# A list schedule in place of the framework's scheduler, for a two-layer hybrid backbone on one core

## The chip, the cores and the metric

The kernel runs on one core of one Trainium2 chip. The metric is the device time of one execution in microseconds (us); three runs of the kernel before gave 1246.17, 1247.41 and 1250.1 us, median 1247.41. The engines are TensorE (PE, with its weight loads as PEld), VectorE (DVE), ScalarE (ACT), GpSimd (POOL) and SyncE (SP, whose queue issues every DMA). Each engine executes its own list of instructions in order; semaphores hold an instruction until what it needs is there.

## The reference

Two layers, 640 tokens (512 of a latent grid, 128 of a prompt), width 1024. In each layer:

```python
def layer(x, cvec, lp, lam_init, cache):
    mod = jax.nn.silu(cvec) @ lp['w_mod'] + lp['b_mod']
    shift, scale, gate = jnp.split(mod[:, None, :], 3, -1)
    h = rms_norm(x, lp['g_pre']) * (1.0 + scale) + shift
    y, new_cache = mixer(h, lp, lam_init, cache)
    return x + gate * rms_norm(y, lp['g_post']), new_cache

def mixer(h, lp, lam_init, cache):   # cut
    (ar, ak, av, awd, aad, ag, bq, bk, bv, bg, cx, cg, dq, dk, dv, dg) = split_cols(h @ lp['w_in'])
    ya = rwkv_branch(...)    # RWKV-7, two directions, state per head
    yb = window_latent(...)  # windowed attention with a sink
    yc = rglru_branch(...)   # convolution, gates, linear recurrence, two directions
    yd = diff_attend(...)    # softmax(q1 k1) - lam * softmax(q2 k2)
    return concat(ya * silu(ag), yb * silu(bg), yc * silu(cg), yd * silu(dg)) @ lp['w_out']
```

## The kernel before

Every projection is a sum of three products of float32r matmuls: activations are held as a high and a low part (`HA`, `HB`), weights too (`WP`, `WQ`, `ZA`, `K`); ACT writes the high part (L515), DVE the difference (L518). All matmuls but the transposes are issued by the helper `mm` (L345).

In a layer the program is written in this order. `fm1`: projections that give the RG-LRU input (tiles 4, 5) and the RWKV inputs (8 to 12). `lru` (L997): convolution, gate products, scans, both directions. `rwkv_norm`, then for direction 0 the stages `pre`, `bonus`, `mats`, `ends`, `inv`, `keys`; five `tm_chunk`s (queries, keys and values of the attentions, with the pieces of the modulation between them); `solve` for direction 0; all stages again for direction 1; the windowed attention with four gate tiles (`fm2`, `E_TILES`, L1656 to L1660); `rwkv_chain` (seven dependent steps on the state) and `rwkv_read`; then the differential attention (`diff`), with four more gate tiles (`F_TILES`), the end of RWKV (`rwkv_out`) and the output weights between its steps; at last `out`. `inv` inverts triangular 32x32 blocks by 31 dependent steps shared by POOL and DVE (L1273, L1275), with a way through DRAM before and after. `diff` works on 4 heads of 5 query tiles: packing (L839, L843, L845), scores, a minimum on DVE (L873), exponentials on ACT (L876), a combination on DVE (L881), transposes (L887) and the product with the values.

Tiles stand in hand-placed slots (`SLOTS`, the `M_...` places): a later tile in the same place waits for the last user of the earlier one. Weights come through two buffers (`raw`, `N_RAW = 2`).

The order on each engine is not the written one. The tile framework's scheduler sets it, from its own estimate of times and from priorities: blocks under `first()` (L1703) are moved ahead by 1000 places, the steps of `window` and `diff` by `WP1` and `DP1` (L1693). So the RG-LRU and the RWKV stages stand beside the first projections.

Of the kernel before, what the change touches and what calls it, by code (L numbers as in the profile page):

```python
# [10 lines left out]
F32 = mybir.dt.float32  # L11
F32R = mybir.dt.float32r
# [9 lines left out]
NT = 5  # L22
# [236 lines left out]
class Net:  # L259
    def __init__(self, tc, es, I, O, dbg=None):  # L260
        self.tc, self.nc, self.I, self.O = tc, tc.nc, I, O
        self.dbg = dbg or {}
        nc = tc.nc
        self.V, self.A, self.G, self.P = nc.vector, nc.scalar, nc.gpsimd, nc.tensor
        self.pool = es.enter_context(tc.tile_pool(name="sb", bufs=1))
        self.ps = es.enter_context(tc.tile_pool(name="ps", bufs=1, space=PSUM))
        self.dram = es.enter_context(tc.tile_pool(name="dr", bufs=1, space=bass.MemoryType.DRAM))
        self.slots = {}
        self.banks = self.ps.tile([128, 8, 512], F32, name="banks")
        self.n = 0  # L270
        self.rot = {}
        self.sm_tag = "sm"
# [5 lines left out]
    def sb(self, shape, tag, bufs=1, dt=F32):  # L278

        self.n += 1  # L280
        return self.pool.tile(list(shape), dt, tag=tag, bufs=bufs, name=f"{tag}_{self.n}")

    def new(self, *slots, dt=F32):

        for k in slots:
            self.n += 1
            self.slots[k] = dt, self.pool.tile([128, round(SLOTS[k] * U)], dt, tag=k, bufs=1, name=f"{k}_{self.n}")

    def at(self, place, shape, dt=F32):

# [228 lines left out]


    def raw(self):
        self.n += 1
        return self.pool.tile([128, RAW], F32, tag="raw", bufs=N_RAW, name=f"raw_{self.n}")

    def weight(self, pieces, hi, lo):

# [1209 lines left out]
```

## Time and profile before

| | |
|---|---|
| median of three runs | 1247.41 us (1246.17 to 1250.1) |
| profiled execution | 1240.3 us, its span 1238.4 us |
| PE busy | 1078.4 us (87%) |
| DVE, ACT, POOL busy | 727.2, 518.0, 385.5 us |
| mean granted TensorE clock | 0.902 of full speed |

The span runs from the first to the last instruction. Busy is the time in which an engine executes something; matmuls are pipelined, so the duration of one matmul in a row is longer than the distance to the next one. PEclk is the granted clock, 1.00 at 2.4 GHz and 0.50 at 1.2 GHz, averaged over a stretch. The views used are: the page's shares, the chain of waits (work followed back from the last instruction), windows (busy time in chosen stretches), and the timeline (instructions in order of time, equal neighbours merged, with the idle time before a row and its releaser in brackets).

### The profile page before, as it was taken

The page shows a single profiled execution, that of the slowest core. Times are in us where ns is not written, and L with a number is a line of the kernel's source. Part 1 is how long each engine was busy: PE and PEld are TensorE (multiplying, and loading weights), DVE is VectorE, ACT ScalarE, POOL GpSimd, SP SyncE. Part 2 cuts the span into 40 slices and gives each one's busy share as a digit, 9 for nine tenths or more (in the row PEclk, how much of TensorE's full clock was granted, in tenths as well). Part 3 has the DMA queues.
Part 4 walks back from the last instruction along what each step waited for, and adds up shares of the span by engine and source line. Part 5 has one row for each costly group of instructions (what it writes and reads, how often), then busy time and mean ns, then how long its engine had stood idle before and what let it go on. Part 6 is the DMA issues. An engine that isn't in the chain of part 4 may idle for free.

```text
span 1238.4 us, 24763 instructions
## 1 busy us (share of the span) xinstructions
PE 1078.4 (87%) x10166; PEld 926.4 (75%) x10166; DVE 727.2 (59%) x1646; ACT 518.0 (42%) x1154; POOL 385.5 (31%) x465
## 2 busy tenths in 40 slices
PE   4999878987999968786998998799889996888796
PEld 3888766877878846565898977698888785666596
DVE  6675784466745467754465277834567548765322
ACT  4467032422344436564145561434234444556310
POOL 0167371115801032200122456713671103310112
PEclk9999889988999987858899998899989997776898
DMA  9412156243231021202121113430223021110111
GB/s 362 165 41 79 48 160 179 83 151 77 81 94 40 26 94 38 69 9 89 70 86 69 52 46 90 152 82 32 71 80 110 24 90 30 39 67 1 38 65 52
DMA packets 60225, 99.97 MB, mean 81 GB/s; under 512 B 30736, under 2 KB 38672, under 8 KB 60112
## 3 DMA queue, kind: packets, MB, share of 16 engines
q1 hardware_dynamic: 60112, 98.39, 24.6%
q8 instruction: 80, 1.31, 0.4%
q14 instruction: 33, 0.27, 0.1%
HBM read 82.90 MB, written 15.47 MB: 79 GB/s over the span
## 4 chain that ended last, share of the span: by engine, by line
PE 57%; DVE 16%; ACT 8%; DMA 7%; issue 6%; POOL 4%; SPq 1%; POOLq 0%; ACTq 0%; DVEq 0%
PE banks L345 50%; PE banks L887 2%; DVE F L1275 2%; ACT FA L876 2%; PE banks L843 2%; DMA F<-inv 1%; DVE F L1273 1%; DVE WP L518 1%; DVE F L1075 1%; PE banks L778 1%; DMA inv<-ZA 1%; DVE dm L873 1%; ACT FA L888 1%; DVE F L839 1%; DMA ZA<-in_w_m 1%
## 5 line engine op out<-in xcount | busy, mean ns | idle before, releaser
L345 PE MATMUL banks<-WP,HA 128*128 128x256 f32 x880 | 178.4, 300 | 18.9 <-DVE WP L518 13.5
L345 PE MATMUL banks<-HA,WP 128*128 128x384 f32 (+1 forms) x768 | 184.6, 321 | 2.3 <-DVE WP L518 1.4
L345 PEld LDWEIGHTS banks<-WP,HA 128*128 128x128 f32 x880 | 146.8, 203 | 24.5 <-DVE WP L518 14.4
L345 PEld LDWEIGHTS banks<-HA,WP 128*128 128x128 f32 x768 | 132.5, 193 | 8.5 <-issue 2.6
L345 PE MATMUL banks<-WP,HB 128*128 128x256 f32 x440 | 130.2, 296 | 0.0
L345 PE MATMUL banks<-HB,WP 128*128 128x256 f32 (+1 forms) x384 | 121.1, 317 | 0.0
L345 PEld LDWEIGHTS banks<-WP,HB 128*128 128x128 f32 x440 | 89.2, 203 | 1.0 <-issue 0.4
L518 DVE TENSOR_TENSOR WP<-raw,WP 128x1024 fp32r<-128x1024 f32 x44 | 60.3, 1373 | 35.4 <-ACT WP L515 34.4
L345 PE MATMUL banks<-FA,F 64*128 64x128 f32 (+3 forms) x768 | 74.6, 298 | 4.8 <-DVE F L1186 3.6
L345 PEld LDWEIGHTS banks<-HB,WP 128*128 128x128 f32 x384 | 74.2, 193 | 1.7 <-DVE gadd L434 0.4
L345 PE MATMUL banks<-WQ,HA 128*128 128x256 f32 x320 | 66.8, 307 | 6.0 <-DVE WQ L518 2.4
L345 PEld LDWEIGHTS banks<-FA,F 64*128 64x128 f32 (+2 forms) x768 | 56.4, 175 | 19.4 <-issue 8.8
L876 ACT ACTIVATE FA<-banks,dm 128x640 f32<-128x640 f32 (+1 forms) x80 | 55.9, 708 | 25.0 <-DVE dm L873 19.4
L515 ACT ACTIVATE WP<-raw 128x1024 fp32r<-128x1024 f32 x46 | 48.3, 1056 | 34.9 <-PE banks L345 16.2
L873 DVE TENSOR_REDUCE dm<-banks 128x2 f32<-128x1280 f32 (+1 forms) x40 | 50.8, 1274 | 18.5 <-PE banks L345 18.5
L345 PEld LDWEIGHTS banks<-WQ,HA 128*128 128x128 f32 x320 | 55.1, 210 | 8.6 <-issue 3.7
L345 PE MATMUL banks<-ZA 96*128 96x512 f32 (+3 forms) x128 | 49.5, 488 | 13.3 <-ACT FA L876 9.8
L843 PE MATMUL banks<-const,F 128*96 128x128 f32 x160 | 34.3, 368 | 27.0 <-DVE F L839 23.6
L698 POOL TENSOR_TENSOR F<-F,mt 128x256 f32<-128x256 f32 (+1 forms) x16 | 14.4, 902 | 136.4 <-DVE mt L696 87.4
L345 PE MATMUL banks<-F,ZA 64*64 64x64 f32 (+2 forms) x1440 | 54.2, 217 | 3.0 <-DMA F<-inv 2.9
L345 PEld LDWEIGHTS banks<-F,ZA 64*64 64x64 f32 (+2 forms) x1440 | 47.7, 130 | 9.5 <-issue 4.4
L887 PE MATMUL banks<-const,FA 128*128 128x128 f32 x168 | 42.9, 351 | 9.7 <-ACT FA L888 8.4
(340 smaller groups left out, 2650.5 us busy)
## 6 DMA issues: line engine op xcount, KB each, us to landing
raw<-in_w_m SPq DMA_DIRECT2D x32, 512.0 KB, 4.3
raw<-in_w_fm SPq DMA_DIRECT2D x30, 512.0 KB, 3.5
raw<-in_w_tm SPq DMA_DIRECT2D x24, 512.0 KB, 3.5
raw<-in_w_o SPq DMA_DIRECT2D x16, 512.0 KB, 3.5
F<-in_x SPq DMA_DIRECT2D x10, 512.0 KB, 5.5
qkv<-F SPq DMA_DIRECT2D x30, 128.0 KB, 1.7
F<-qkv SPq DMA_DIRECT2D x6, 640.0 KB, 5.2
ZA<-in_w_m SPq DMA_DIRECT2D x6, 512.0 KB, 10.5
```

The source lines that it names most:

```text
L345: self.P.matmul(out, lhsT, rhs, start=start, stop=stop)
L515: self.A.activation(hi, x, AF.Copy)
L518: (E or self.V).tensor_tensor(lo, x, hi.bitcast(F32), op=ALU.subtract)
L698: self.G.tensor_tensor(x, x, g, op=ALU.mult)
L778: P.transpose(pt[:, b * 128:(b + 1) * 128], eh[:, b * 128:(b + 1) * 128], self.ident)
L839: V.scalar_tensor_tensor(tmp[:, :, m, lo, :], x, c, tmp[:, :, m, 0, :].bitcast(F32), op0=ALU.mult, op1=ALU.subtract)
L843: P.transpose(reg[0:96, j * 128:j * 128 + 128], tmp[:, i, m].rearrange("p a d -> p (a d)").bitcast(F32), self.ident)
L873: V.tensor_reduce(nm, sc, axis=AX.X, op=ALU.min)
L876: A.activation(e[:, m, :], sc[:, m, :], AF.Exp, bias=nm[:, m:m + 1], scale=-1.0, accum_out=s1 if m else s0)
L887: P.transpose(ps[:, k:k + 128], e[:, 0, k0 + k:k0 + k + 128], self.ident)
L888: A.activation(pt[:, k0:k0 + w], ps, AF.Copy)
L1275: E.tensor_tensor(N[:, rows, cs], N[:, rows, cs], t, op=ALU.subtract)
```

## The change

The program that is written stays the same: the same 10,855 instructions with the same operands, buffers and dependencies. New is who orders them. `plan` builds the program once in advance, takes its instructions and dependencies, adds a gate wherever a buffer is reused, and hands them to `_list_schedule`. That one gives each instruction a length by a table of its own (`_length`), ranks it by the longest way from it to the end, and lets each engine take the best-ranked one that is ready. `follow` then ties each instruction to its predecessor on the engine, so that the framework has no choice left. The hand-set priorities thereby lose their effect.

Two features are in the change's name. Small products are dear: matmuls with at most 64 rows are counted by their own formula. And a matmul with at most 64 rows next to one of more (`half`) costs `TURN`; the schedule stays with its kind while another of that kind ranks within `STAY`.

```diff
+SEEN = {"PE": 0.18, "DVE": 0.06, "Activation": 0.06, "Pool": 0.07}
+NEXT = {"DVE": 0.05, "Activation": 0.05, "Pool": 0.05}
+def _length(i):
...
+    if e == "PE":
+        n, m, k = _width(ins[0]), _width(ins[1]), list(ins[0].ap)[0][1]
+        if ins[0].dtype == F32R or i.is_transpose:
+            return 0.33 if k == 1 else max(0.11, 0.00043 * n + 0.01)
+        if k > 64:
+            return 0.1 if m <= 32 else (0.06 if n <= 64 else 0.113) if m <= 64 else max(0.22, 0.00155 * n)
+        return 0.0016 * n if m > 64 else 0.034 if m <= 32 else max(0.055, 0.0009 * n)
...
+TURN = 0.1
+STAY = 2.0
+def _list_schedule(names, engine, length, deps, size, half):
...
+    for n in reversed(todo):
+        own = length[n] + (2.0 + size[n] / 220 if engine[n] == "SP" else 0.0)
+        tail[n] = own + max((tail[s] + seen(n, s) for s in succ[n]), default=0.0)
...
+        t, k = min((idle[e] if here[e] else max(idle[e], come[e][0][0]), k) for k, e in enumerate(queues) if here[e] or come[e])
...
+        if e == "PE":
+            if half[n] != turned:
+                other = [x for x in here[e] if half[x[1]] == turned and x[0][0] < rank[n][0] + STAY]
...
+                else:
+                    t += TURN
...
+        if e == "SP":
+            link = max(link, t + 1.2) + size[n] / 220
+            end = link + 0.6
...
+def follow(tc, order):
...
+        if e in last:
+            tc.add_manual_dep(i, last[e].name, mybir.DependencyInfo(mybir.DependencyClass.NoSync, mybir.DependencyReason.DATA),
+                              reason="plan")
+        last[e] = i
 def body(tc, I, O, dbg=None):
+    order = plan(I, O)
     with ExitStack() as es:
         Net(tc, es, I, O, dbg).run()
+    follow(tc, order)
```

Three places show what moves. In the kernel after, the same lines have numbers higher by 5 or 7 (L345 is L352, L518 is L525, L843 is L848, L1064 is L1069).

First, DVE in the first projections of layer 0, before. `raw` are weights on their way into `WP` and `WQ`; L988 is the RG-LRU's convolution, L1064 its first gate product (`FA`); `raw_896` belongs to `fm1` tile 12.

```order
L518 TENSOR_TENSOR WP_85<-raw_786,WP_85 128x8x128
L988 SCALAR_TENSOR_TENSOR F_77<-F_77,par_75 128x643
L518 TENSOR_TENSOR WP_85<-raw_790,WP_85 128x8x128
L988 SCALAR_TENSOR_TENSOR F_77<-F_77,par_75 128x643
L1094 TENSOR_SCALAR K_80<-K_80,par_75 128x640
L988 SCALAR_TENSOR_TENSOR F_77<-F_77,par_75 128x643
L518 TENSOR_TENSOR WQ_86<-raw_896,WQ_86 128x1024
L1094 TENSOR_SCALAR K_80<-K_80,par_75 128x640
L1064 SCALAR_TENSOR_TENSOR FA_78<-FA_78,F_77 128x512
```

The same place on DVE after; `raw_950` to `raw_1521` are the weights of the first two `tm_chunk`s.

```order
L525 TENSOR_TENSOR WQ_86<-raw_896,WQ_86 128x1024
L1045 TENSOR_SCALAR lsm_515<-par_75 128x4
L1099 TENSOR_SCALAR K_80<-K_80,par_75 128x640 x2
L796 TENSOR_SCALAR sink_130_3505<-par_75 128x4
L525 TENSOR_TENSOR WP_85<-raw_950,WP_85 128x1024
L525 TENSOR_TENSOR WP_85<-raw_954,WP_85 128x1024
L525 TENSOR_TENSOR WQ_86<-raw_1517,WQ_86 128x1024
L525 TENSOR_TENSOR WQ_86<-raw_1521,WQ_86 128x1024
L1069 SCALAR_TENSOR_TENSOR FA_78<-FA_78,F_77 128x512
```

Four more weight splits now stand ahead of the first gate product of the RG-LRU.

Second, PE at the start of the differential attention of layer 0, before. L843 are the transposes of its packing, `ZA` rows its scores, L887 the transposes of its exponentials, `K_80,FA_78` the steps of `rwkv_chain` and `rwkv_read`.

```order
L843 MATMUL banks<-const_66,F_77 96x128 x2
L345 MATMUL banks<-K_80,FA_78 64x64 x16
L345 MATMUL banks<-ZA_4248 128x256
L345 MATMUL banks<-K_80,FA_78 64x64 x4
L887 MATMUL banks<-const_66,FA_78 128x128
L345 MATMUL banks<-WQ_1999,FA_78 64x64 x8
L345 MATMUL banks<-FA_78,F_77 64x128 x2
L843 MATMUL banks<-const_66,F_77 96x128 x4
L345 MATMUL banks<-ZA_4248 128x512
L843 MATMUL banks<-const_66,F_77 96x128 x12
```

The same place on PE after. The rows with `WP_85` are matmuls of the gate tiles `fm2`.

```order
L848 MATMUL banks<-const_66,F_77 96x128
L352 MATMUL banks<-HB_84,WP_85 128x384
L352 MATMUL banks<-HA_83,WP_85 128x384
L848 MATMUL banks<-const_66,F_77 96x128
L352 MATMUL banks<-HA_83,WP_85 128x384
L352 MATMUL banks<-ZA_4248 128x384
L352 MATMUL banks<-ZA_4248 128x512
L352 MATMUL banks<-HB_84,WP_85 128x384
L352 MATMUL banks<-ZA_4248 128x128
L352 MATMUL banks<-ZA_4248 128x256
L352 MATMUL banks<-HA_83,WP_85 128x384 x2
```

Gate matmuls that stood before the differential attention now stand between its own.

Third, DVE a little later, before. L1446 and L1448 belong to `rwkv_out`, L839 to the packing of the next head, L873 to the scores.

```order
L1422 TENSOR_TENSOR WQ_1999<-WQ_1999,banks 128x2x64 x2
L1446 TENSOR_REDUCE sm_4516<-WQ_1999 128x20
L1447 TENSOR_SCALAR sm_4516<-sm_4516 128x20
L1448 TENSOR_TENSOR WQ_1999<-WQ_1999,sm_4516 128x1280
L839 SCALAR_TENSOR_TENSOR F_77<-F_77 128x5x32
L873 TENSOR_REDUCE dm_4381<-banks 128x2
```

DVE after, from the same step of `rwkv_read` (L1427) on; L525 and L710 are a weight split and a gate of `fm2`.

```order
L1427 TENSOR_TENSOR WQ_1999<-WQ_1999,banks 128x8x64
L878 TENSOR_REDUCE dm_4381<-banks 128x2
L844 SCALAR_TENSOR_TENSOR F_77<-F_77 128x5x32 x2
L525 TENSOR_TENSOR WP_85<-raw_3937,WP_85 128x1024
L710 SCALAR_TENSOR_TENSOR K_80<-K_80,banks 128x384
L844 SCALAR_TENSOR_TENSOR F_77<-F_77 128x5x32 x2
```

`rwkv_out` has gone from the head of the stage (its first operation now stands 28 rows further down, behind five score minima); a weight split and gate operations have come in.

## Rows read from the trace of the kernel before

**Rows 1.** The page: busy time, and the chain that ended last.
```profile
PE 1078.4 (87%) x10166; PEld 926.4 (75%) x10166; DVE 727.2 (59%) x1646; ACT 518.0 (42%) x1154; POOL 385.5 (31%) x465
...
PE 57%; DVE 16%; ACT 8%; DMA 7%; issue 6%; POOL 4%; SPq 1%; POOLq 0%; ACTq 0%; DVEq 0%
```

**Rows 2.** Windows by stage: start:end, length, busy by engine (instructions), PEclk, DMA, GB/s.
```profile
0.00:31.00 31.00, 13.86 (x115) 9.63 (x116) 19.98 (x97) 15.19 (x28) 0.56 (x6) 1.00 0.95 362
31.00:152.00 121.00, 115.80 (x807) 101.61 (x806) 80.80 (x158) 58.79 (x97) 55.19 (x42) 0.94 0.23 85
152.00:213.00 61.00, 48.60 (x545) 40.13 (x545) 37.72 (x118) 16.09 (x40) 28.30 (x54) 0.89 0.58 160
213.00:283.00 70.00, 65.00 (x912) 55.07 (x904) 38.39 (x70) 24.38 (x47) 10.55 (x11) 0.93 0.36 117
283.00:362.00 79.00, 67.77 (x601) 61.60 (x601) 52.50 (x108) 26.52 (x67) 45.93 (x90) 0.96 0.34 92
362.00:440.00 78.00, 76.74 (x1071) 65.75 (x1066) 39.69 (x108) 34.27 (x89) 7.58 (x10) 1.00 0.13 44
440.00:592.00 152.00, 115.83 (x819) 86.96 (x815) 98.89 (x181) 81.30 (x200) 25.41 (x12) 0.77 0.17 56
592.00:771.00 179.00, 167.80 (x1218) 155.48 (x1219) 101.20 (x210) 78.48 (x147) 72.11 (x60) 0.96 0.19 67
771.00:827.00 56.00, 47.61 (x511) 43.99 (x511) 34.01 (x102) 17.15 (x39) 29.67 (x54) 0.91 0.43 123
827.00:902.00 75.00, 71.20 (x960) 63.66 (x954) 39.68 (x63) 27.91 (x57) 38.04 (x49) 0.98 0.19 60
902.00:964.00 62.00, 57.97 (x513) 51.25 (x512) 40.59 (x122) 25.19 (x66) 25.45 (x53) 0.94 0.31 86
964.00:1020.00 56.00, 54.79 (x843) 46.46 (x841) 29.14 (x74) 26.97 (x69) 6.72 (x8) 1.00 0.15 51
1020.00:1174.00 154.00, 122.02 (x898) 92.84 (x897) 98.32 (x188) 79.11 (x198) 26.78 (x13) 0.74 0.11 35
```

**Rows 3.** Chain of waits: start us, us, what (a gapless run of projections).
```profile
665.35 43.31 PE banks L345 x292
```

**Rows 4.** Timeline of PE: start us, us, engine line op out<-in xcount; last gate product of `lru`, first `mats`.
```profile
104.37 1.24 PE L345 MATMUL banks<-F,FA 128*128 128x512 f32 x4
...
139.61 3.52 PE L345 MATMUL banks<-FA,F 64*128 64x128 f32 x24 [0.83 <-DVE F L1184]
```

**Rows 5.** Chain of waits around the first `inv`: start us, us, what.
```profile
154.72 2.45 DMA inv<-ZA
157.31 5.29 DMA F<-inv
...
189.06 0.22 DVE F L1275
...
195.38 7.37 DMA raw<-in_w_m
```

**Rows 6.** Timeline of PE when the first `inv` comes back.
```profile
209.00 1.47 PE L345 MATMUL banks<-F,ZA 32*32 32x32 f32 x80
```

**Rows 7.** Timeline of DVE and PE at the start of `diff`.
```profile
453.02 3.50 DVE L1448 TENSOR_TENSOR WQ<-WQ,sm 128x1280 f32<-128x1280 f32 x1
...
456.45 3.01 DVE L839 SCALAR_TENSOR_TENSOR F<-F 128x160 fp32r<-128x160 f32 x1
...
459.51 1.52 PE L843 MATMUL banks<-const,F 128*96 128x128 f32 x6 [6.38 <-DVE F L839]
```

**Rows 8.** Timeline of PE: a change from 128 rows to 64.
```profile
379.59 0.33 PE L345 MATMUL banks<-HB,WP 128*128 128x384 f32 x1
379.76 0.34 PE L345 MATMUL banks<-HA,WP 128*128 128x384 f32 x1
380.03 0.27 PE L345 MATMUL banks<-F,ZA 64*64 64x64 f32 x1
```

**Rows 9.** Timeline of PE: a weight not yet there.
```profile
271.21 0.51 PE L345 MATMUL banks<-WP,HA 128*128 128x256 f32 x2 [1.50 <-ACT WP L515]
```

More of the change, by code (lines that the diff above doesn't have):

```diff
@@ L1 @@
+import heapq
 import itertools
@@ L271, in __init__ @@
         self.rot = {}
+        self.rings = {}
         self.sm_tag = "sm"
@@ L278, in sb, with tile @@
     def sb(self, shape, tag, bufs=1, dt=F32):
+        return self.tile(shape, dt, tag, bufs)
+    def tile(self, shape, dt, tag, bufs, pool=None):
         self.n += 1
-        return self.pool.tile(list(shape), dt, tag=tag, bufs=bufs, name=f"{tag}_{self.n}")
+        name = f"{tag}_{self.n}"
+        t = (pool or self.pool).tile(list(shape), dt, tag=tag, bufs=bufs, name=name)
+        self.rings.setdefault(tag, (bufs, []))[1].append(t.name)
+        return t
     def new(self, *slots, dt=F32):
         for k in slots:
-            self.n += 1
-            self.slots[k] = dt, self.pool.tile([128, round(SLOTS[k] * U)], dt, tag=k, bufs=1, name=f"{k}_{self.n}")
+            self.slots[k] = dt, self.tile([128, round(SLOTS[k] * U)], dt, k, 1)
     def at(self, place, shape, dt=F32):
@@ L521, in raw @@
     def raw(self):
-        self.n += 1
-        return self.pool.tile([128, RAW], F32, tag="raw", bufs=N_RAW, name=f"raw_{self.n}")
+        return self.tile([128, RAW], F32, "raw", N_RAW)
     def weight(self, pieces, hi, lo):
@@ L592, in tm_alloc @@
         self.bv = kb[:, 1, :].rearrange("p (i n) -> p i n", i=NT)
-        self.n += 1
-        self.qkv = self.dram.tile([3, 128, NT, 256], F32, tag="qkv", bufs=2, name=f"qkv_{self.n}")
+        self.qkv = self.tile([3, 128, NT, 256], F32, "qkv", 2, self.dram)
         self.SV = self.at(M_SV, [128, NT, 2, 4, 64])
@@ L1251, in rwkv_inv @@
         self.n += 1
-        xd, nd, ntd = (self.dram.tile([80, 32, 32], F32, tag=f"inv{k}", bufs=2, name=f"inv{k}_{self.n}") for k in range(3))
+        xd, nd, ntd = (self.tile([80, 32, 32], F32, f"inv{k}", 2, self.dram) for k in range(3))
         quad = [(p, b, slice(20 * (2 * p + b), 20 * (2 * p + b) + 20), slice(64 * (1 - p) + 32 * b, 64 * (1 - p) + 32 * b + 32))
@@ L1712, in stage, with _width, _engine @@
         getattr(self, "rwkv_" + name)(d)
+ENGINES = "PE", "DVE", "Activation", "Pool", "SP"
+SEEN = {"PE": 0.18, "DVE": 0.06, "Activation": 0.06, "Pool": 0.07}
+NEXT = {"DVE": 0.05, "Activation": 0.05, "Pool": 0.05}
+def _width(a):
+    return math.prod(k for _, k in list(a.ap)[1:])
+def _engine(i):
+    return str(i.engine).split(".")[-1]
+def _length(i):
+    e, kind = _engine(i), type(i).__name__[4:]
+    ins = [a for a in i.ins if hasattr(a, "ap") and hasattr(a, "memref")]
+    if e == "PE":
[5 more added lines that the diff above has]
+        return 0.0016 * n if m > 64 else 0.034 if m <= 32 else max(0.055, 0.0009 * n)
+    n = max(_width(a) for a in (*i.outs, *ins))
+    if e == "Activation":
+        return 0.21 + 0.0008 * n
+    if e == "Pool":
+        return 0.24 + 0.0021 * n if kind == "TensorTensor" else 0.28 + 0.00083 * n if kind != "Memset" else 0.11 + 0.00082 * n
+    if any(a.memref.startswith("banks") for a in (*i.outs, *ins)):
+        return 0.16 + 0.00107 * n
+    return 0.29 + 0.0012 * n if sum(2 * _width(a) > n for a in ins) > 1 else 0.22 + 0.0006 * n
@@ new lines @@
+TURN = 0.1
+STAY = 2.0
+def _list_schedule(names, engine, length, deps, size, half):
+    succ, left = {n: [] for n in names}, {}
+    for n in names:
+        left[n] = len(deps[n])
+        for x in deps[n]:
+            succ[x].append(n)
+    seen = lambda n, s: 0.0 if engine[n] == engine[s] != "SP" else SEEN.get(engine[n], 0.0)
+    todo, tail, free = [n for n in names if not left[n]], {}, dict(left)
+    for n in todo:
+        for s in succ[n]:
+            free[s] -= 1
+            if not free[s]:
+                todo.append(s)
+    for n in reversed(todo):
+        own = length[n] + (2.0 + size[n] / 220 if engine[n] == "SP" else 0.0)
+        tail[n] = own + max((tail[s] + seen(n, s) for s in succ[n]), default=0.0)
+    rank = {n: (-tail[n], k) for k, n in enumerate(names)}
+    queues, turned = ENGINES + (None,), False
+    idle, link, ready = dict.fromkeys(queues, 0.0), 0.0, dict.fromkeys(names, 0.0)
+    come, here, out = {e: [] for e in queues}, {e: [] for e in queues}, []
+    for n in names:
+        if not left[n]:
+            heapq.heappush(come[engine[n]], (0.0, rank[n], n))
+    while len(out) < len(names):
+        t, k = min((idle[e] if here[e] else max(idle[e], come[e][0][0]), k) for k, e in enumerate(queues) if here[e] or come[e])
+        e = queues[k]
+        while come[e] and come[e][0][0] <= t:
+            _, r, n = heapq.heappop(come[e])
+            heapq.heappush(here[e], (r, n))
+        _, n = heapq.heappop(here[e])
+        if e == "PE":
+            if half[n] != turned:
+                other = [x for x in here[e] if half[x[1]] == turned and x[0][0] < rank[n][0] + STAY]
+                if other:
+                    x = min(other)
+                    here[e].remove(x)
+                    heapq.heapify(here[e])
+                    heapq.heappush(here[e], (rank[n], n))
+                    n = x[1]
+                else:
+                    t += TURN
+            turned = half[n]
+        out.append(n)
+        end = t + length[n]
+        if e:
+            idle[e] = end + NEXT.get(e, 0.0)
+        if e == "SP":
+            link = max(link, t + 1.2) + size[n] / 220
+            end = link + 0.6
+        for s in succ[n]:
+            ready[s] = max(ready[s], end + seen(n, s))
+            left[s] -= 1
+            if not left[s]:
+                heapq.heappush(come[engine[s]], (ready[s], rank[s], s))
+    return out
@@ new lines, in plan @@
+def plan(I, O):
+    import concourse.bacc as bacc
+    nc = bacc.Bacc("TRN2", target_bir_lowering=False, num_devices=1)
+    I, O = ({n: nc.dram_tensor(f"{p}_{n}", a.shape, F32, kind=k).ap() for n, a in x.items()}
+            for p, x, k in (("in", I, "ExternalInput"), ("out", O, "ExternalOutput")))
+    with tile.TileContext(nc, schedule_with_timeline_sim=True) as tc:
+        with ExitStack() as es:
+            net = Net(tc, es, I, O)
+            net.run()
+        trace = list(nc.cur_bb.bb.instructions)
+    names = [i.name for i in trace if _engine(i) in ENGINES and i.outs and hasattr(i.outs[0], "ap")]
+    place = {i.name: k for k, i in enumerate(trace)}
+    known = set(names)
+    trace = {i.name: i for i in trace}
+    engine = {n: _engine(trace[n]) for n in names}
+    length = {n: 0.08 if engine[n] == "SP" else _length(trace[n]) for n in names}
+    half = {n: engine[n] == "PE" and list(trace[n].ins[0].ap)[0][1] <= 64 for n in names}
+    size = {n: math.prod(k for _, k in trace[n].outs[0].ap) / 256 if engine[n] == "SP" else 0.0 for n in names}
+    deps = {n: {d for d, _ in nc.dependency_edges(n)} & known for n in names}
+    users = {}
+    for n in names:
+        for t in {a.memref for a in (*trace[n].ins, *trace[n].outs) if hasattr(a, "memref")}:
+            users.setdefault(t, []).append(n)
+    for bufs, tiles in net.rings.values():
+        tiles = [t for t in tiles if t in users]
+        for old, new in zip(tiles, tiles[bufs:]):
+            gate = "after " + old
+            names.append(gate)
+            engine[gate], length[gate], size[gate], deps[gate] = None, 0.0, 0.0, set(users[old])
+            for n in users[new]:
+                deps[n].add(gate)
+    return [place[n] for n in _list_schedule(names, engine, length, deps, size, half) if n in place]
@@ L1715, in body @@
+def follow(tc, order):
+    trace = list(tc.nc.cur_bb.bb.instructions)
+    last = {}
+    for k in order:
+        i = trace[k]
+        e = _engine(i)
+        if e in last:
+            tc.add_manual_dep(i, last[e].name, mybir.DependencyInfo(mybir.DependencyClass.NoSync, mybir.DependencyReason.DATA),
+                              reason="plan")
+        last[e] = i
 def body(tc, I, O, dbg=None):
+    order = plan(I, O)
     with ExitStack() as es:
         Net(tc, es, I, O, dbg).run()
+    follow(tc, order)
```

## The prediction

> **What bounds the kernel now.** I read the page's shares first, then windows cut at the program's own seams (the first row of `mats`, the end of `inv`, the first packing of `diff`), then the chain and the timeline at the seams. The page [rows 1] says that PE is busy 87% of the span, yet only 57% of the chain that ended last lies on PE; 16% lies on DVE, 8% on ACT, 7% on DMA. So PE is the bound for most of the time, and about an eighth of the span is lost where it waits for a chain through other engines. The windows [rows 2] show where. They are, per layer, (a) first projections with the RG-LRU up to the first `mats`, (b) `mats`, `ends` and `inv` of direction 0, (c) to the `mats` of direction 1, (d) to the end of its `inv`, (e) to the first packing of `diff`, (f) `diff`; a tail closes layer 1. The reader is to compare length and PE's busy time, first of the five. In (e) of layer 0 PE is busy 76.74 of 78 us and in (c) 65.00 of 70: these are PE's. In (f) it is busy 115.83 of 152 at a granted clock of 0.77, and in layer 1 122.02 of 154 at 0.74: here PE waits, a head's score, minimum (DVE), exponential (ACT), transpose follow one another, and the clock falls. In (b) it is busy 48.60 of 61: the inverse goes through DRAM and 31 steps on DVE and POOL [rows 5].
>
> So the kernel has two stages with nothing for PE to do for 36 and 32 us, and right ahead of each a stage that is full of PE work. What the change is worth depends on whether the work is carried from one to the other.
>
> **What the change moves.** No instruction goes or comes. Counting PE's matmuls by these stages in the order before and after gives, for layer 0: a 738 to 925, b 393 to 313, c 528 to 396, d 514 to 471, e 637 to 479, f 588 to 814. For layer 1: a 1097 to 1082, b 423 to 288, c 588 to 512, d 424 to 474, e 481 to 479, f 636 to 814. Of the 384 gate matmuls (`fm2`) of a layer, 48 stood inside `diff` before, and 274 do now. A projection's matmul costs 43.31 / 292 = 0.148 us where PE runs without a gap [rows 3]; that is my price for each one moved.
>
> (a), layer 0. PE gets 187 matmuls more: 187 x 0.148 = 27.7 us. Its work was 13.86 + 115.80 = 129.7 us, and the first 31 us have 31.00 - 13.86 = 17.1 us in which it waits for the first data. 129.7 + 27.7 + 17.1 = 174.5 us. The other bound is the RG-LRU. Its last gate product starts at 104.37 and the first `mats` at 139.61, 35.2 us later [rows 4]; the seam lies 12.4 us after that, at 152. In the order after, about 115 us of PE's work stand ahead of that gate product (it and its kind come some 28 us later, behind four more weight splits on DVE); with the 17.1 us it starts no earlier than 132. 132 + 34 + 12 = 178. I take 178, from 174.5 to 185: +26 us, a price to be earned back later.
>
> (b), layer 0. The chain `mats`, write, read, 31 steps, DRAM and back sets the end; the steps end at 189.28, and PE takes the result at 209.00 [rows 5, 6], since the transfer of other weights (7.37 us) and projections stand in between. The 80 matmuls that go (11.8 us) were part filling, part in the way. If all were filling, the stage keeps 61 us; if the last stretch goes from 20 us to 12, 53. I take 55: -6.
>
> (c), layer 0: 132 fewer, -19.5 us, so 50.5 to 70; PE was busy 65 of 70, so I take nearly all less the idle that a shorter stage brings out: 56, -14. (d): 43 fewer, -6.4; 72.6 to 79, I take 73. (e): 158 fewer, -23.4; 54.6 to 78, near its low end since PE was busy 98% of it: 57, -21.
>
> (f), layer 0: 226 more, +33.4 us. They fit into the 36.2 us in which PE waits, if they stand where it waits and not where a head's chain needs it: 115.83 + 33.4 = 149.2 us at the clocks of before. DVE has 98.89 and ACT 81.30 us of work in 152, so neither sets the end, even with the gates' share. `rwkv_out` no longer stands ahead of the first packing on DVE (3.50 us for its last step alone, then packing, and PE waits 6.38 us [rows 7]). I take 148, from 138 to 160: from below by the clock (first rival), from above by 8 us of waits that the fixed order puts in front of the heads. The heads' values wait for the four `E_TILES`' matmuls, which share a bank with them; those have now moved into the same stage, which is what could put it at 160.
>
> Layer 0: 178 + 55 + 56 + 73 + 57 + 148 = 567, before 592.
>
> Layer 1 by the same prices: a 179 to 176 (15 fewer, -2.2); b 56 to 54 (the same chain through DRAM, less in its way; 51 to 56); c 75 to 65 (76 fewer, -11.2; 63.8 to 75); d 62 to 64 (50 more, mostly small, into 4 us of idle time; 62 to 68); e 56 to 55 (2 fewer); f 154 to 150 (178 more, 26.3 us into 32 us of waiting; 140 to 162); the tail stays, 1238.4 - 1174 = 64.4. Sum 628, before 646.4.
>
> The turns from 128 rows to 64. One is seen as 0.27 us between starts where 0.17 is usual [rows 8]: 0.10 us. Counted in both orders, there are 388 before and 306 after: 82 x 0.10 = 8.2 us. About half lie where PE is the bound: -4, from 0 to -8.
>
> 567 + 628 - 4 = 1191 us of span, against 1238.4. The profiled execution of before took 1240.3 us, 1.9 more than its span; the median of the three runs, 1247.41, lies 9.0 above that span. Adding the 9.0 gives 1200 us. The main case's own range, with its terms' bounds taken together but not all on one side, is 1170 to 1225.
>
> **Rivals.** First, the same mechanism with the clock as a gain. With gate matmuls between the heads PE hardly pauses in `diff`. Before, the clock was 0.77 where PE was busy 115.83 of 152, and 1.00 in the stage ahead, busy 76.74 of 78 [rows 2]. A mean of 0.77 is 46% of the time at 1.2 GHz. Had all of it run at 2.4 GHz, PE's own part would be at best 115.83 x 0.77 = 89 us, plus 33.4 is 122; halfway between 122 and 152 is about 138, and by the same way 140 in layer 1 (122.02 x 0.74 + 33.4 = 124). That is 20 us less: 1180, and down to 1155 if the heads' chain allows it. Against it: the heads' chain, not PE's rate, sets this stage, and 99 us of DVE in it don't get shorter. The Trainium skill, "TensorE: Matmul & The Clock Gate", section "What's actually happening", says that the slow clock is the default and that activity releases it; the two stages' clocks agree with it (0.77 and 1.00), and by it alone the time would be this rival's, 1180.
>
> Second, about even. (c) and (e) are shortened by half of what I say, since DVE and POOL work in them too: c 63, e 67.5 and c of layer 1 70, together +22; `diff` takes 160 in both layers, +22. 1200 + 44 = 1244, from 1240 to 1250.
>
> Third, slower: one mechanism, PE's fixed order at the wrong moment. The order was made with lengths and transfer times from a table (220 bytes per ns, where the first 31 us moved 362 GB/s [rows 2]). If an instruction at the head of PE's list isn't ready, everything behind waits, though it is ready. The trace has such a wait: 1.50 us for a weight at 271.21 [rows 9]. The program loads 102 pieces of weights through `raw`, and in `diff` gate matmuls now stand between a head's transposes and scores, behind weights that DVE splits between its minima. Price: 1.5 us for each piece that is late. It decides from about 31 late pieces on, 47 us, the whole forecast gain; with half of them late, 50 x 1.5 = 75 us, the time is 1275, and this case goes from 1250 on. For it: the table's rate is far from the one seen, and four weight splits stand ahead of the RG-LRU's first gate product. Against it: before, such waits are few where PE is dense, 1.3 us in all of (e), where it was busy 98%. The Trainium skill, in the same page's section "Step-by-step: what each phase is for", says that PE may fetch a weight load forward, but that matmuls run in program order. The wait of 1.50 us agrees, and this rule speaks against the change wherever a gate's weight is late.
>
> That the change doesn't do what it says is out: the order shows the moves.
>
> **How the numbers follow.** The main case has 0.55, the clock rival 0.13, the even one 0.15, the slower one 0.17. A run of this kernel can be told from no change at about 0.3%, 3.7 us. Faster: 0.55 + 0.13 and a good third of the even case, 0.74; same 0.07; slower 0.19, with the rest of the even case. The range takes in the clock rival's low end and the even case: 1152 to 1250.
>
> **What the profile after would show.** Right: first `mats` at about 165 and seam (a) at 178; `inv`'s result on PE some 55 us later; first packing of `diff` at about 419, not 440; PE busy 145 or more of 150 in both `diff` windows, its clock above 0.85 there; PE's share of the chain above 65%. Wrong: `diff` longer than 155 with PE idle in it (then the third rival's waits are to be seen in front of scores and transposes, released by DVE's splits or ACT); a first packing no earlier than 435 (then c to e were not PE's); seam (a) past 185 (the RG-LRU is later than counted); or the same lengths at a clock of 1.00, in which case the clock was free and I priced PE wrongly.

## The result, and the profile after

The changed kernel takes 1214.98 us, median of four runs (1207.87 to 1216.64); the kernel before, run beside it, 1248.76. The ratio is 0.9714, interval 0.9663 to 0.9764. The forecast was 1200 in a range of 1152 to 1250: the direction and the main case hold, of the forecast 47 us 34 came. The profiled execution took 1215.67 us, its span 1213.8, so the spans differ by 24.6 us and the medians by 33.8: the profiled run of before was one of its shorter ones.

The page of the kernel after: busy time, and the chain of waits (it could be followed back to 917.10 us only, so its shares end at 24%).

```profile
PE 1068.7 (88%) x10166; PEld 916.2 (75%) x10166; DVE 739.7 (61%) x1646; ACT 515.9 (43%) x1154; POOL 373.8 (31%) x465
...
PE 17%; DVE 3%; issue 2%; ACT 2%; POOL 0%; POOLq 0%; ACTq 0%; DVEq 0%
```

Of the span's 24.6 us, 9.7 are PE's busy time (1078.4 before [rows 1]) and the rest its idle time; the granted clock hardly moved (0.902 to 0.904). PE holds 17 of the chain's 24%, 71%.

The windows of the kernel after, cut at the same seams as [rows 2]; the first two together are stage (a) of layer 0. Columns: start:end, length, busy of PE, PEld, DVE, ACT, POOL (instructions), PEclk, DMA share, GB/s.

```profile
0.00:31.00 31.00, 16.59 (x133) 10.71 (x134) 16.13 (x67) 15.99 (x28) 0.58 (x7) 1.00 0.95 373
31.00:186.00 155.00, 147.25 (x1025) 126.95 (x1029) 82.37 (x183) 65.22 (x108) 52.43 (x43) 0.90 0.30 100
186.00:244.00 58.00, 39.08 (x449) 31.68 (x447) 40.18 (x135) 14.30 (x35) 25.76 (x54) 0.79 0.50 149
244.00:297.00 53.00, 47.92 (x747) 38.16 (x741) 30.81 (x52) 19.48 (x38) 13.40 (x11) 0.94 0.22 68
297.00:377.00 80.00, 68.41 (x604) 60.47 (x603) 59.24 (x128) 28.31 (x75) 46.60 (x90) 0.82 0.30 84
377.00:426.00 49.00, 49.00 (x868) 41.10 (x866) 27.83 (x82) 24.88 (x68) 2.56 (x4) 0.94 0.15 52
426.00:579.00 153.00, 136.19 (x1032) 109.91 (x1027) 107.41 (x192) 85.83 (x213) 30.37 (x18) 0.92 0.16 51
579.00:754.00 175.00, 167.53 (x1184) 155.31 (x1185) 97.41 (x200) 79.84 (x145) 72.71 (x59) 0.95 0.22 76
754.00:811.00 57.00, 35.65 (x422) 30.28 (x419) 39.31 (x97) 15.49 (x31) 25.05 (x54) 0.76 0.44 119
811.00:870.00 59.00, 55.93 (x824) 49.37 (x822) 33.28 (x68) 20.99 (x48) 12.23 (x11) 0.97 0.13 41
870.00:950.00 80.00, 68.83 (x608) 61.30 (x608) 54.77 (x124) 28.47 (x76) 46.45 (x90) 0.85 0.30 87
950.00:999.00 49.00, 49.00 (x866) 41.11 (x865) 27.32 (x81) 24.61 (x67) 2.57 (x4) 0.94 0.14 49
999.00:1152.00 153.00, 136.48 (x1033) 110.22 (x1027) 107.37 (x192) 85.83 (x213) 29.90 (x18) 0.91 0.15 49
```

| stage (us) | before | forecast | after | | before, layer 1 | forecast | after |
|---|---|---|---|---|---|---|---|
| a | 152 | 178 | 186 | | 179 | 176 | 175 |
| b | 61 | 55 | 58 | | 56 | 54 | 57 |
| c | 70 | 56 | 53 | | 75 | 65 | 59 |
| d | 79 | 73 | 80 | | 62 | 64 | 80 |
| e | 78 | 57 | 49 | | 56 | 55 | 49 |
| f | 152 | 148 | 153 | | 154 | 150 | 153 |

The shape is the forecast one: (a) of layer 0 pays, (c) and (e) earn. In (e) PE is busy for the whole 49.00 us. What the reader is to see beside it: in both `diff` stages the clock rose, 0.77 to 0.92 and 0.74 to 0.91, PE is busy 136 instead of 116 and 122 us, and yet the stage isn't shorter; in (a), (b), (d) and (e) of layer 0 the clock fell, from 0.94, 0.89, 0.96 and 1.00 to 0.90, 0.79, 0.82 and 0.94. And (d) of layer 1 is longer, with POOL busy 46.45 us in it, where it was 25.45. In [rows 2] its first seam, 902, stood 3 us behind the end of the last `mats`, at 898.8: by that (c) of layer 1 was 72 long before and (d) 65, so (d) grew by 15 us. Cut there, the window of before is:

```profile
898.80:964.00 65.20, 61.17 (x532) 54.01 (x532) 43.36 (x125) 25.19 (x66) 28.66 (x56) 0.95 0.33 91
```

PE is busy 8 us longer in (d) after, at a clock of 0.85 instead of 0.95, and idle 7 us longer.

What has changed in (d) is POOL's list. Its timeline in layer 1 after: L1278 and L1280 are the inverse's steps, L586 begins the rotation of queries and keys for the differential attention (L586 to L591).

```profile
879.51 0.23 POOL L1278 TENSOR_TENSOR KPP<-WQ,F 80x23 f32<-80x23 f32 x1
...
901.02 0.85 POOL L586 TENSOR_TENSOR F<-F,const 128x256 f32<-128x256 f32 x1 [4.69 <-ACT F L662]
...
910.78 0.73 POOL L586 TENSOR_TENSOR F<-F,const 128x256 f32<-128x256 f32 x1 [2.89 <-ACT F L662]
...
914.19 0.73 POOL L586 TENSOR_TENSOR F<-F,const 128x256 f32<-128x256 f32 x1 [1.45 <-ACT F L662]
...
929.45 0.24 POOL L1280 TENSOR_TENSOR F<-F,KPP 80x23 f32<-80x23 f32 x1
```

The same steps before, first and last.

```profile
910.17 0.24 POOL L1273 TENSOR_TENSOR KPP<-WQ,F 80x23 f32<-80x23 f32 x1 [3.67 <-DMA WQ<-inv]
...
935.29 0.23 POOL L1275 TENSOR_TENSOR F<-F,KPP 80x23 f32<-80x23 f32 x1
```

50.2 us from the first step to the last, against 25.4: the rotations stand between the steps, and three of them wait 9.0 us for ACT with ready steps behind them. The first of these waits comes from PE: the copy on ACT that it needs (L662) stood waiting for a projection.

```profile
900.56 0.39 ACT L662 ACTIVATE F<-banks 128x256 f32<-128x256 f32 x1 [5.51 <-PE banks L352]
```

### The profile page after: what moved, and what is told of

It reads as the page before. It is cut to its first block, busy times and chain, and to the rows that moved or that the text cites. A ratio compares the mean times of both kernels' runs of the same rounds, so it can differ in the third digit from the quotient of the medians.

```text
span 1213.8 us, 24805 instructions
## 1 busy us (share of the span) xinstructions
PE 1068.7 (88%) x10166; PEld 916.2 (75%) x10166; DVE 739.7 (61%) x1646; ACT 515.9 (43%) x1154; POOL 373.8 (31%) x465
## 5 line engine op out<-in xcount | busy, mean ns | idle before, releaser
L352 PE MATMUL banks<-WP,HA 128*128 128x256 f32 x880 | 197.0, 309 | 23.6 <-DVE WP L525 18.2
L352 PE MATMUL banks<-HA,WP 128*128 128x384 f32 (+1 forms) x768 | 208.5, 344 | 7.3 <-DVE mt L701 5.0
L352 PEld LDWEIGHTS banks<-WP,HA 128*128 128x128 f32 x880 | 153.8, 208 | 35.0 <-DVE WP L525 19.6
L352 PEld LDWEIGHTS banks<-HA,WP 128*128 128x128 f32 x768 | 141.8, 204 | 16.4 <-DVE mt L701 5.8
L352 PE MATMUL banks<-HB,WP 128*128 128x384 f32 (+1 forms) x384 | 127.9, 342 | 0.5 <-DVE HB L525 0.4
L352 PE MATMUL banks<-WP,HB 128*128 128x256 f32 x440 | 127.1, 304 | 0.0
L352 PEld LDWEIGHTS banks<-WP,HB 128*128 128x128 f32 x440 | 88.6, 208 | 3.1 <-issue 2.5
L525 DVE TENSOR_TENSOR WP<-raw,WP 128x1024 fp32r<-128x1024 f32 x44 | 54.1, 1234 | 50.8 <-ACT WP L522 42.9
L352 PE MATMUL banks<-WQ,HA 128*128 128x256 f32 x320 | 78.9, 308 | 6.4 <-ACT WQ L522 5.5
L352 PEld LDWEIGHTS banks<-HB,WP 128*128 128x128 f32 x384 | 77.6, 205 | 4.9 <-issue 2.6
L352 PE MATMUL banks<-FA,F 64*128 64x128 f32 (+3 forms) x768 | 70.5, 283 | 7.8 <-DVE F L1191 4.1
L352 PEld LDWEIGHTS banks<-WQ,HA 128*128 128x128 f32 x320 | 59.4, 207 | 10.6 <-ACT WQ L522 6.4
L352 PEld LDWEIGHTS banks<-FA,F 64*128 64x128 f32 (+2 forms) x768 | 50.7, 162 | 21.4 <-issue 10.3
L352 PE MATMUL banks<-F,ZA 64*64 64x64 f32 (+2 forms) x1440 | 58.6, 220 | 1.7 <-ACT K L1238 1.7
L352 PEld LDWEIGHTS banks<-F,ZA 64*64 64x64 f32 (+2 forms) x1440 | 50.9, 133 | 9.2 <-issue 3.0
L352 PE MATMUL banks<-WQ,HB 128*128 128x256 f32 x160 | 47.1, 302 | 0.0
L352 PE MATMUL banks<-raw,cs 128*32 128x256 f32 x256 | 27.6, 453 | 20.3 <-DVE gg L455 12.9
L352 PE MATMUL banks<-HA,WQ 128*128 128x384 f32 (+1 forms) x192 | 45.4, 315 | 0.0
```

The source lines that it names most:

```text
L352: self.P.matmul(out, lhsT, rhs, start=start, stop=stop)
L525: (E or self.V).tensor_tensor(lo, x, hi.bitcast(F32), op=ALU.subtract)
```

## The experiments

Each was timed in five rounds beside the kernel before; as the level moves a little from one set to the next, ratios to the kernel before are compared (0.01 is 12.5 us).

**1. No charge for changing rows.**

```diff
-TURN = 0.1
-STAY = 2.0
+TURN = 0.0
+STAY = 0.0
```

> The changed kernel with TURN and STAY at 0: the list schedule takes no notice of the number of rows. PE then changes between at most 64 and more rows 610 times instead of 306. Theory (a change costs PE 0.10 us, rows 8): 304 x 0.10 = 30 us more of PE busy time, some three quarters of it where PE is the bound, so 1235 to 1245 us, and PE busy about 1099. Rival (a change is covered by the weight load or by waits): 1211 to 1219 us, PE busy within 5 us of 1069.

Measured: 1294.44 us, ratio 1.0398 (1.0356 to 1.0440), slower than before the change. PE busy is 1150.3 us, 81.6 more. Stage (e) of layer 0, which is PE's alone, in this kernel:

```profile
395.00:461.30 66.30, 65.45 (x896) 51.52 (x894) 26.68 (x82) 25.42 (x66) 2.03 (x4) 0.89 0.12 43
```

It holds 493 matmuls with 97 changes of rows, where the changed kernel has 478 with 32 in 49.0 us: (17.3 - 15 x 0.148) / 65 = 0.23 us a change, by an estimate that prices the 15 as projections. Layer 1, at nearly the clock of the changed kernel (0.95 and 0.94), gives 0.21 (19 matmuls and 53 changes more):

```profile
1016.40:1079.50 63.10, 62.26 (x899) 49.74 (x898) 29.53 (x88) 25.70 (x66) 2.39 (x4) 0.95 0.12 44
```

Over the whole kernel, with the same matmuls, at a mean clock of 0.896 and 0.904, it is 81.6 / 304 = 0.27 us of PE's busy time. The theory's direction holds, and what a further change costs is more than twice its price. The single pair wasn't misread: from start to start at the full clock, the trace of the changed kernel has a step to at most 64 rows 0.11 us longer than an unchanged step behind a matmul of the same shape (130 steps), and a step back 0.12 (123 steps). But the steps without a change of rows are longer too in run 1: in (e) of layer 1 those from one record of a small matmul to the next take 0.042 us on average, in the changed kernel 0.035, and those between large ones 0.086 and 0.075; why was not taken apart.

And rows are not all that switches. By the same reckoning a step between matmuls of 128 rows is 0.14 us longer where the columns of the array change (128 to 64 or 32, or back: the second number in `128*64`; 227 steps). Counted by rows and columns, the order changes 579 times before and 596 after. So `TURN` charges about half of the changes, and in all they have not become fewer.

**2. Small products planned at half their price.**

```diff
-            return 0.1 if m <= 32 else (0.06 if n <= 64 else 0.113) if m <= 64 else max(0.22, 0.00155 * n)
-        return 0.0016 * n if m > 64 else 0.034 if m <= 32 else max(0.055, 0.0009 * n)
+            return 0.5 * (0.1 if m <= 32 else (0.06 if n <= 64 else 0.113) if m <= 64 else max(0.22, 0.00155 * n))
+        return 0.5 * (0.0016 * n if m > 64 else 0.034 if m <= 32 else max(0.055, 0.0009 * n))
```

> The changed kernel with the four prices of small f32 products halved in the table. 384 changes of rows instead of 306 and somewhat more work in the inverse's stages and in diff. Theory (order hardly depends on these prices, only the turns cost): 78 x 0.10 = 8 us, 1218 to 1226. Rival (the prices decide: with products planned at half, what stands behind them is planned too early and PE waits at its head): 1235 or more.

Measured: 1280.55 us, ratio 1.0287 (1.0249 to 1.0325): the rival. PE busy is only 15.5 us up (1084.2), so most of the loss is waiting. The longest entries of PE's waits (engine line waited for: us in total, times, longest):

```profile
PE banks L352 <- DVE WQ L525: 20.4, 1, 20.4
PE banks L352 <- ACT F L763: 15.2, 11, 5.0
PE banks L352 <- DVE WP L525: 13.5, 6, 3.2
```

One weight is late by 20.4 us, with PE's list held behind it. Over the kernel PE waits 42.8 us for weights here, 29.5 in the changed kernel and 21.9 before. So a fixed order is worth what its table is worth: the third rival's mechanism is real, but late weights make only 13 us of this loss, and the other waits were not taken apart.

**3. Gate products ahead of `diff`, as before the change.**

```diff
...
+    for l in range(L):
+        gates = [n for n in known if stage.get(n) == (l, "fm2") and engine[n] == "PE"]
+        gates = sorted(gates, key=place.get)[:336]
+        for n in known:
+            if stage.get(n) == (l, "dpk0_") and engine[n] == "PE":
+                deps[n].add(gates[-1])
```

> The changed kernel, but in each layer the first 336 matmuls of fm2 must stand ahead of diff's first packing, as before the change; 48 are in diff instead of 274. Theory (gate matmuls in diff stand where PE waits for a head's chain, so they are nearly free there): 226 x 0.148 = 33 us a layer come back ahead of diff, diff hardly gets shorter (145 to 153): 1255 to 1280 us. Rival (diff is now full of PE work, and shrinks by what leaves it): diff 120 to 130 us, the total 1210 to 1230.

Measured: 1274.27 us, ratio 1.0218 (1.0179 to 1.0256), as the theory says of the total; `diff` shrinks further than its 145 to 153, and less than the rival's 120 to 130. Its windows (d), (e) and (f) of layer 0, and (f) of layer 1:

```profile
287.00:387.60 100.60, 89.39 (x794) 76.72 (x795) 67.43 (x146) 38.35 (x98) 48.16 (x94) 0.92 0.27 77
387.60:457.40 69.80, 69.80 (x903) 54.94 (x904) 29.97 (x80) 23.79 (x57) 4.20 (x5) 1.00 0.14 48
457.40:597.00 139.60, 117.85 (x802) 86.05 (x800) 102.34 (x178) 79.47 (x200) 25.21 (x13) 0.77 0.13 43
...
1061.70:1205.00 143.30, 121.96 (x802) 88.25 (x800) 102.47 (x178) 79.39 (x200) 25.22 (x13) 0.74 0.12 40
```

(d) and (e) grow by 41 us, `diff` shrinks by 13 and 10. So 226 gate products cost 10 to 13 us inside `diff` and some 41 ahead of it (33 by their price; the other 8 were not taken apart). Two things I had not separated are seen here: with as many matmuls as before (589), the list schedule's `diff` takes 140 and 143 instead of 152 and 154 us, so the new order inside it gained 11 to 12, and the gates then gave it back. Which part of that order gains (`rwkv_out` no longer ahead of the first packing, or the order of the heads) no run separates. And the clock in `diff` goes with PE's filling: 0.77 and 0.74 without the gates, 0.92 and 0.91 with them.

**4. and 7. Only some engines follow the plan.** The tie in `follow` for all but PE (run 4, shown), and for PE alone (run 7, with `==` for `!=`):

```diff
-        if e in last:
+        if e in last and e != "PE":
```

> The changed kernel with the planned order tied on every engine but PE; PE's order is the framework's own choice around it (364 changes of rows, 264 gate matmuls in diff, LRU gate products earlier by 50 places). Theory (the stages' contents make the gain, and they follow from the others' order): 58 turns, 6 us: 1217 to 1226. Rival (PE's list in detail makes the gain): 1232 or more.

> The changed kernel with the planned order tied on PE alone; DVE, ACT, POOL and SP are ordered by the framework around it. Theory (PE's list carries the gain, since leaving PE free cost 146 us): 1215 to 1235. Rival (an order pays only when all engines follow the same plan): 1280 or more.

Measured: 1360.98 us, ratio 1.0901 (1.0846 to 1.0956), and 1312.79, ratio 1.0536 (1.0483 to 1.0589). Both theories fall and both times lie where the rivals put them; PE's list in detail matters, but alone it doesn't carry the gain. Half a plan is worse here than none. `diff` of layer 0 with PE free:

```profile
456.30:644.90 188.60, 151.72 (x1021) 121.29 (x1019) 107.49 (x193) 85.64 (x213) 29.60 (x18) 0.81 0.14 47
```

36 us longer than under the whole plan, with nearly the same instructions. Which pair of engines crosses there was not taken apart.

**5. and 6. The late RG-LRU.** In 5 the planner's rate becomes 400 bytes per ns; in 6 the last gate product of the RG-LRU is ranked 40 us higher.

```diff
-        own = length[n] + (2.0 + size[n] / 220 if engine[n] == "SP" else 0.0)
+        own = length[n] + (2.0 + size[n] / 400 if engine[n] == "SP" else 0.0)
...
-            link = max(link, t + 1.2) + size[n] / 220
+            link = max(link, t + 1.2) + size[n] / 400
```

```diff
-        tail[n] = own + max((tail[s] + seen(n, s) for s in succ[n]), default=0.0)
+        tail[n] = own + lead.get(n, 0.0) + max((tail[s] + seen(n, s) for s in succ[n]), default=0.0)
...
+        lead[max((n for n in known if stage.get(n) == (l, "lru") and engine[n] == "PE"), key=place.get)] = 40.0
```

> The changed kernel with 400 instead of 220 bytes per ns for transfers in the planner. In layer 0 the first stage holds 836 PE matmuls instead of 925, the LRU's last gate product stands at place 674 instead of 709, and 15 to 65 more matmuls are in the next three stages. Theory (the matmuls in the first stage are only moved ahead and come back later; the late LRU sets no end): first stage 186 to 170, the total 1205 to 1219. Rival (the first stage's 34 us are a loss made by the wrong rate, and the rest keeps its length): 1180 to 1195 us.

> The changed kernel with 40 us added to the rank of each layer's last RG-LRU gate product and so of all that it needs: it stands at PE place 543 instead of 709, while the first stage keeps 900 of 925 matmuls. Forecast's step (LRU's last product plus 34 plus 12 us sets the end of the first stage): first stage about 165, total 1195 to 1205. Rival (PE's own work sets that end, since PE is busy 147 of its 155 us): first stage 182 to 188, total 1211 to 1222.

Measured: 1201.09 us, ratio 0.9635 (0.9589 to 0.9681), and 1208.46, ratio 0.9714 (0.9673 to 0.9754). In run 6 PE's first `mats`, after and in run 6:

```profile
172.34 1.22 PE L352 MATMUL banks<-FA,F 64*128 64x128 f32 x6
```

```profile
169.91 0.71 PE L352 MATMUL banks<-FA,F 64*128 64x128 f32 x6
```

The row with the RG-LRU's last products starts 12 us earlier (115.7 against 128.1), the first `mats` only 2 us, with no wait right before them in either kernel, and the ratio is the same. (a) ends at 180, with 25 matmuls fewer in it: far from the 165 of the forecast's step, a little below the rival's range, as is the time. So the RG-LRU doesn't set the end of (a); PE's own list does. In run 5 the rate takes 8 us off (a) (177.5), gives 18 back in (c) (70.9), and wins 9 and 10 in the two `diff` stages (144.2, 142.8). Its time lies between what the theory and its rival gave; against the changed kernel the intervals just overlap.

**9. POOL's rotations behind the inverse.**

```diff
...
+        step = max((n for n in known if stage.get(n) == (l, "rwkv_inv1_") and engine[n] == "Pool"), key=place.get)
+        for n in known:
+            if stage.get(n) == (l, "tm_chunk") and engine[n] == "Pool":
+                deps[n].add(step)
```

> The changed kernel, but the 40 POOL operations of each layer that rotate queries and keys (L586 to L591) must stand behind POOL's last step of the second inverse. Theory (stage d of layer 1 became 80 instead of 66 us because these rows, waiting 4.69, 2.89 and 1.45 us for ACT, stand between POOL's steps of the inverse): stage d 63 to 70 us in both layers, and what is put off makes stage e longer (609 matmuls instead of 479, 130 x 0.148 = 19 us): total 1210 to 1235. Rival (d is set by PE, busy 69 of 80 us, or by DVE): d stays at 75 to 82, e grows by the same 19 us, total 1250 or more.

Measured: 1231.01 us, ratio 0.9855 (0.9826 to 0.9884). Stages (d) and (e) of both layers:

```profile
291.50:353.00 61.50, 47.79 (x507) 44.26 (x506) 44.22 (x84) 19.57 (x41) 44.95 (x89) 0.87 0.41 117
353.00:433.00 80.00, 79.35 (x1065) 62.41 (x1061) 42.09 (x131) 35.27 (x102) 2.90 (x6) 0.95 0.15 51
871.00:933.00 62.00, 50.49 (x505) 46.05 (x505) 45.39 (x80) 19.38 (x41) 44.35 (x89) 0.84 0.38 105
933.00:1013.00 80.00, 79.35 (x1068) 62.41 (x1064) 42.22 (x131) 35.39 (x104) 3.13 (x6) 0.95 0.15 52
```

(d) falls from 80 to 62 in both layers. POOL's first and last step in layer 1:

```profile
882.51 0.24 POOL L1278 TENSOR_TENSOR KPP<-WQ,F 80x23 f32<-80x23 f32 x1 [6.86 <-DMA WQ<-inv]
...
904.83 0.23 POOL L1280 TENSOR_TENSOR F<-F,KPP 80x23 f32<-80x23 f32 x1
```

The steps take 22.6 us instead of 50.2: what stands between them on POOL made them long. But (d) also holds 71 and 65 matmuls fewer (400 for 471, 409 for 474), some 10 us by the price of [rows 3], so how much of the 18 us is the chain's alone isn't shown. (e) pays 31: 130 matmuls, 19.2 us as projections (48 of them are small), and 41 more changes of rows, (31.1 - 19.2) / 41 = 0.29 each by this estimate. The cure costs more than it brings.

**8., 10., 11. and 12. The table's other numbers.** Run 8 has 340 bytes per ns and `TURN` 0.15; run 10 has 400 and

```diff
-    length = {n: 0.08 if engine[n] == "SP" else _length(trace[n]) for n in names}
+    length = {n: 0.08 if engine[n] == "SP" else _length(trace[n]) * (1.1 if engine[n] == "PE" else 1.0) for n in names}
```

Run 11 has 400 and `TURN` 0.25, run 12 `TURN` 0.25 alone:

```diff
-TURN = 0.1
+TURN = 0.25
```

> The changed kernel with 340 bytes per ns and TURN at 0.15 (a change of rows before 64x64 products shows 0.15 between starts more than without one). 306 changes of rows, first stage 848 matmuls. If the rate is the table's one wrong number: 1190 to 1210. If it makes no difference: 1211 to 1219.

> The planner with 400 bytes per ns and all PE lengths times 1.1 (stage e holds PE's work alone and took 49.0 us). Theory (the remaining waits at the heads of the lists come from a PE that is later than planned): 1180 to 1197 us. Rival (the order no longer hangs on it): 1197 to 1208, as with the rate alone (1201.09).

> The planner with 400 bytes per ns and TURN 0.25 (from stage e of the first experiment: 65 changes more made it 17 us longer, 0.26 each). 284 changes of rows instead of 324 with the rate alone. Theory (0.25 each): 40 x 0.25 = 10 us, 1188 to 1197. Rival (differences of this size are the accident of one order): 1197 to 1212.

> The changed kernel with TURN 0.25 alone, the rate at 220. The order has 310 changes of rows, not fewer than the 306 of the changed kernel, 286 to 289 gate matmuls in diff and 35 PE matmuls fewer in stage e of layer 0. Theory (0.25 us for each change that is really in the list, whatever the planner charges): 1209 to 1222 us. Rival (a dearer charge makes a better order by itself, as it seemed with the rate): 1195 to 1208.

Measured: run 8, 1210.94 us, ratio 0.9696 (0.9639 to 0.9754), not to be told from the changed kernel; run 10, 1216.36, 0.9741 (0.9711 to 0.9771): a slower PE in the table takes back what the rate alone had gained, outside both ranges; run 11, 1195.35, 0.9582 (0.9552 to 0.9612); run 12, 1204.93, 0.9663 (0.9623 to 0.9703), in the rival's range, but its interval overlaps that of the changed kernel. Run 11 is the best version here and beats both kernels; its page:

```profile
PE 1057.4 (88%) x10166; PEld 903.2 (76%) x10166; DVE 741.0 (62%) x1646; ACT 514.8 (43%) x1154; POOL 367.1 (31%) x465
```

Its window of stage (e), layer 0:

```profile
382.00:421.30 39.30, 38.97 (x771) 32.11 (x770) 22.77 (x72) 18.96 (x52) 0.00 (x0) 1.00 0.13 45
```

PE is busy 11 us less than in the changed kernel. Between run 5 and run 11 stage (e) loses 33 matmuls (4.9 us), 16 changes and 7.3 us in all: 0.15 a change. Rate and charge bring 0.8 and 0.5 per cent by themselves, too little to tell from the changed kernel; together, 1.3 per cent, they can be told. That the truer numbers are the cause isn't shown: runs 8 and 10 raise the rate too, and gain nothing on the changed kernel.

## Why the prediction was right, and where its sizes were off

**Carrying work from (c) and (e) to `diff`.** Right, and it is the gain: taking that one move back (run 3) makes the kernel slower than before. The size of (c) and (e) was 3 to 8 us too careful a stage. In (e) of layer 0 the changes of rows fell from 47 to 32, which I had priced apart and too low. In (e) of layer 1 the term that was mis-sized is the count: 480 and 478 matmuls by the order, but those of more than 64 rows went from 268 to 214 and the smaller ones from 212 to 264, and I gave all the price of a projection.

**`diff` at 148 and 150.** It came out at 153. I priced 226 gates at -4 a layer; run 3 shows them at +10 to +13, hidden in the sum by 11 to 12 us that the new order inside `diff` brings: two errors that cancel, so that the 153 is near by luck. PE is busy 136 us of it, not the 145 of 150 that I named as the sign.

**The clock rival.** Its premise came true (0.92, 0.91) and its price did not: the stage with the gates in it is no shorter at the faster clock. Whether that clock saved anything inside it isn't shown, since no run has the gates there at the lower one. The sum of this rival for layer 1 also took 33.4 us of gates, where 178 matmuls are 26.3. The mean over the kernel stayed where it was (0.902, 0.904), since other stages lost clock. The rule that activity releases the clock (the Trainium skill, "TensorE: Matmul & The Clock Gate", "What's actually happening") agrees with `diff`'s rise from 0.77 to 0.92, where PE's busy share rose from 76% to 89%; the time that it would give by itself, 1180, did not come.

**(a) of layer 0 at 178.** It is 186, with the first `mats` at 172.3 and not 165; the stages behind it kept these 7 us, and the first packing of `diff` came at 426, not 419. The two bounds were 174.5 by PE and 178 by the RG-LRU; run 6 shows that PE's was the right one, and it was too low: PE is busy 163.8 us instead of my 157.4, at a clock of 0.90 instead of 0.94, and idle 22.2 instead of 17.1. So the sign "seam (a) past 185" came, but not for the reason I gave it, a late RG-LRU. In [rows 4] I also took the second row of `mats` for the first. The first stood at 138.07, and PE did wait for DVE there, as it no longer does after:

```profile
138.07 0.71 PE L345 MATMUL banks<-FA,F 64*128 64x128 f32 x8 [3.56 <-DVE F L1186]
```

**(d) of layer 1 at 64.** The step that failed most, 16 us, of which 3 are my seam. I counted its PE work alone, and called the 50 matmuls more mostly small, where the order has 116 of at most 64 rows both before and after; [rows 2] already showed POOL busy 45.93 us in (d) of layer 0 and 25.45 in layer 1, and the order moved the rotations of layer 1 from (c) to (d). Run 9 takes them out from between the steps and (d) is 62. In layer 0 they stood there before the change too; that stage came out at 80 instead of 73, and run 9 gives 61.5.

**The turns.** Priced at 0.10 us each, which is right for the single step; runs 1, 9 and 11 give 0.15 to 0.29 for a further change where PE is the bound. The 82 fewer are so by rows alone; with the columns there are 17 more.

**From span to median.** By spans I forecast 1191 and it was 1213.8, 23 us off. The 9.0 us I added from the profiled run of before to the median were only 1.2 in the kernel after, which hid 8 of them. That is luck, and so is part of the 23: the stages miss by 16 us too low to 8 us too high and partly cancel.

The third rival came in small with this table: PE waits 29.5 us for weights in 13 waits, before 21.9 in 10, which is 8 us more; 47 would have eaten the whole gain. Run 2 shows how dear a wrong table can be, 71 us in all.

## What to carry to other kernels

A list schedule that every engine follows paid here, with a table that was good enough on the bound engine, and it couldn't be applied by halves: runs 1, 2, 4 and 7 differ from it in one detail each (the charge, the small products, who follows), and all are slower than the order it replaced. To forecast a move of work between stages, count every engine's share in both stages, and the kinds of the matmuls, not only the bound engine's number: an in-order helper engine that gets other work between the steps of a chain lengthens the chain, here from 25.4 to 50.2 us. And read the price of a switch (here of matmul rows) from a stage that is full, by two orders with different counts, not from one pair of rows, and let the count take in every kind of it.

## What the runs showed of the hardware

In the changed kernel, a step between matmuls of at most 64 and of more rows is 0.11 to 0.12 us longer than an unchanged one, in both directions, and with 128 rows a change of the columns lengthens it too (0.14 us). A further change of rows cost a full stage more than the single step: 0.21 to 0.23 us by run 1 and 0.15 to 0.29 by runs 9 and 11, all estimates.

The granted clock went with PE's filling in `diff` (0.77 at 117.85 busy of 139.60 us in run 3, 0.92 at 136.19 of 153.00), but the busy share of a stage doesn't give it: (d) of layer 0 had 0.96 before at 67.77 busy of 79.00 [rows 2], and 0.82 after at 68.41 of 80.00. And a stage can begin at the clock that the one ahead of it left. Stage (e) of the changed kernel is busy throughout, behind (d) with its pauses; its mean of 0.94 is a start at 1.2 GHz (0.50) and 2.4 GHz from then on:

```profile
377.00:382.50 5.50, 5.50 (x23) 4.83 (x22) 2.77 (x6) 1.98 (x7) 1.19 (x2) 0.50 0.00 0
382.50:426.00 43.50, 43.50 (x847) 36.27 (x845) 25.06 (x77) 22.90 (x61) 1.37 (x2) 1.00 0.17 58
```
